# Seven products of quarter sums for the channel mixer's second product, with operand sums made on GpSimd

## The chip, the cores and the metric

The kernel runs on one core of a Trainium2 chip. The metric is the device time of one execution in microseconds (us); lower is better. A core has five engines with instruction streams of their own: PE (TensorE: matmuls, with PEld for its weight loads), DVE (VectorE), ACT (ScalarE), POOL (GpSimd) and SP (SyncE, which here issues DMAs). Work passes between them through SBUF, through PSUM (eight banks that matmuls accumulate in) and through DRAM.

## The reference, cut to what matters

The reference is one layer of a diffusion backbone: two token mixers (latent attention and a bidirectional recurrence), a merge, a channel mixer and a final norm, all in float32. The change touches the channel mixer, on 1024 rows of 1024 channels with an inner width of 2816:

```
u = h @ w_up                                  # 1024 x 5632
a, g = split(u, 2)
a = dwconv(a, ffn_conv_w, ffn_conv_b, 1, 1)   # three rows wide, each channel by itself
y = (silu(a) * g) @ w_down                    # 2816 -> 1024: the "second product"
x = x + g2 * y
out = rms_norm(x, final_g)
```

## The kernel before, in words

**Precision.** A float32 operand is split into a high part, rounded to fp32r by a copy on ACT, and a low part, the difference, by a subtraction on DVE (`split`, lines 119 to 122, and `high` and `low`, lines 1507 to 1518). Each product is then three matmuls: high by high, high by low, low by high.

**The first product** (h @ w_up) takes the 22 column tiles f of a and the 22 of g together, in a loop over f. It is already made of seven products of sums of quarters (Strassen's scheme in Winograd's form): for each f the left operands are sums of quarters of the weights (`wsum`, on DVE), the right operands are sums of quarters of h, made once, and seven products of 12 matmuls each (`times`, line 1548), in the order 1, 6, 5, 2, 7, 4, 3, accumulate in three PSUM banks. DVE and ACT combine the banks (`c_first`, `c_11` on ACT, and five sums `c_u2`, `c_u3`, `c_22`, `c_21`, `c_12` on DVE, line 1559) into `cpg[f]`, whose first half is a and whose second is g. While PE works on f, ACT and DVE finish f-1: convolution (`e_center`, `e_sides`, lines 1580 to 1585), `e_silu`, the gating (`e_gated`, line 1592), the split of the gated tile (`e_high`, `e_low`, lines 1596 and 1599), and a store of both parts to DRAM (`act_d`, issued on POOL, line 1600). They also prepare the operands for f+1. The order of all instructions of PE, DVE, ACT and SP is written out by hand in `channel_mixer`; each engine works through its own in that order, and what an engine waits for delays all that stands behind it on that engine. POOL has nothing to do in this stage but to issue the stores.

**The second product** (`Down`) works in two groups of four row tiles. For each group it goes through the 22 tiles f of the inner width: a step fetches half of the split activation and a weight tile (on SP), multiplies the weights by the gate row g2 (line 1801), splits them (line 122), and runs 24 matmuls (line 1812: four row tiles, two column halves, three part products) into eight PSUM banks. Three steps are prepared ahead. The last three f of each group are run tile by tile, so that the sum with x2 (line 1820), the norm and the store of a row tile (`final`) begin while PE is at the next tile. The second group's first tile uses the banks of the first group's first tile.

Of the kernel before, what the change touches and what calls it, by code (L numbers as in the profile page):

```python
# [106 lines left out]
class Block:  # L107
# [1378 lines left out]
    def setup_up(self):  # L1486
        self.ra, self.rg, self.s3, self.op, self.banks, self.p1, self.cpg, self.bt = ({} for _ in range(8))
        self.ups = None
        self.act_d = [self.tc.dram_tile([P, 2, T], F32, name=f"actd{f}") for f in range(NF)]
# [65 lines left out]
    def c_11(self, f):  # L1555
        self.nc.scalar.activation(self.cpg[f][:, 0, :512], self.bank(f, 1), AF.Copy)
# [4 lines left out]
    def c_u2(self, f):  # L1561
        self.c_sum(self.cpg[f][:, 0, 512:], self.p1[f], self.bank(f, 6))
# [4 lines left out]
    def c_22(self, f):  # L1567
        self.c_sum(self.cpg[f][:, 1, 512:], self.p1[f], self.bank(f, 5))

    def c_21(self, f):  # L1570
        self.c_sum(self.cpg[f][:, 1, :512], self.p1[f], self.bank(f, 4))

    def c_12(self, f):
        c = self.cpg[f][:, 0, 512:]
        self.c_sum(c, c, self.bank(f, 3))


    def e_center(self, f):
        self.ta = self.stage("ta")
        self.nc.scalar.activation(self.ta, self.cpg[f][:, 0, :], AF.Identity, bias=self.vec("fb", f), scale=self.vec("fw", 3 * f + 1))  # L1580

    def e_sides(self, f):
        c, ta, stt = self.cpg[f][:, 0, :], self.ta, self.nc.vector.scalar_tensor_tensor
# [6 lines left out]
    def e_gated(self, f):  # L1590
        g = self.cpg[f][:, 1, :]
        self.nc.vector.tensor_tensor(g, g, self.ta, op=OP.mult)

    def e_high(self, f):
        self.act = self.ups.tile([P, 2, T], F32R, tag="act", bufs=2, name=f"act{f}")
        self.nc.scalar.activation(self.act[:, 0, :], self.cpg[f][:, 1, :], AF.Copy)

    def e_low(self, f):
        self.nc.vector.tensor_tensor(self.act[:, 1, :], self.cpg[f][:, 1, :], self.act[:, 0, :].bitcast(F32), op=OP.subtract)  # L1599
        self.nc.gpsimd.dma_start(self.act_d[f], self.act.bitcast(F32))  # L1600

    def channel_mixer(self):
        tc, nc, a = self.tc, self.nc, self.a
        right_ctx, ups_ctx, down = ExitStack(), ExitStack(), Down(self)
        with tc.manual_schedule(engines=self.engines | {mybir.EngineType.SP}):
            cp = right_ctx.enter_context(self.pool("cpg", side="right"))
            h0, h1 = self.hf
            high, low, wsum = self.high, self.low, self.wsum

            def new_cpg(f):  # L1610
                self.cpg[f] = cp.tile([P, 2, T], F32, tag="cpg", bufs=2, name=f"cpg{f}")
# [16 lines left out]
            def first_sum(f):  # L1628
                new_cpg(f)
                self.p1[f] = self.cpg[f][:, 1, :512]  # L1630
                self.c_first(f)
# [53 lines left out]
            self.e_high(0)  # L1685
            low(2, 2)
            low(2, 7)
            self.e_low(0)
            high(2, 4)
            low(2, 4)  # L1690
            for f in range(2, NF):
# [5 lines left out]
                if not new:  # L1697
                    down.fetch_weights(0)
                    down.fetch_weights(1)
# [10 lines left out]
                if f > 2:  # L1710
                    first_sum(f)
                self.e_sides(f - 1)
                self.e_silu(f - 1)
# [4 lines left out]
                self.c_u2(f)  # L1718
                if new:
                    wsum(n, 7)  # L1720
                self.e_gated(f - 1)

                self.times(f, 2)
                self.e_high(f - 1)
# [4 lines left out]
                self.e_low(f - 1)  # L1729

                self.times(f, 7)
                self.c_11(f)
                if new:
# [20 lines left out]

            for n in range(3):
                down.fetch(n)
            down.fetch_weights(2)
# [7 lines left out]
            self.e_sides(f)  # L1765
            self.e_silu(f)
            down.prepare(3)
            self.e_gated(f)
            self.e_high(f)
            self.e_low(f)  # L1770
            ups_ctx.close()
            self.b_ctx.close()
            with self.pool("x2") as xp, self.pool("dn_ps", space=PSUM) as pp:
                down.run(xp, pp)
            right_ctx.close()


class Down:


    AHEAD, REST = 3, 3

    def __init__(self, b):
        self.b, self.nc = b, b.nc
        self.steps = [(g, f) for g in range(2) for f in range(NF)]
        self.acts, self.wds, self.raws = {}, {}, {}

    def fetch_weights(self, n):
        if n < len(self.steps):
            self.raws[n] = self.b.fetch(self.b.a["wdn"][self.steps[n][1]])  # L1790

    def fetch(self, n):
        if n < len(self.steps):
            g, f = self.steps[n]
            self.acts[n] = self.b.big(f"act{n}").rearrange("p (a b) -> p a b", a=2)
            self.nc.sync.dma_start(self.acts[n].bitcast(F32), self.b.act_d[f][:, :, g * 512:(g + 1) * 512])

    def prepare(self, n):
        if n < len(self.steps):
            raw = self.raws.pop(n)  # L1800
            self.nc.vector.tensor_tensor(raw, raw, self.b.g2r, op=OP.mult)
            wd = self.wds[n] = [self.b.big(f"wd{n}_{p}") for p in range(2)]
            self.b.split(raw, *wd)
            self.fetch_weights(n + 3)
            self.fetch(n + 3)

    def times(self, n, t, ps, cs=(0, 1)):
        f, act, wd = self.steps[n][1], self.acts[n], self.wds[n]
        for c in cs:
            p = ps[c]  # L1810
            for j, (rp, wp) in enumerate(((0, 0), (0, 1), (1, 0))):
                self.nc.tensor.matmul(p, act[:, rp, t * P:(t + 1) * P], wd[wp][:, c * 512:(c + 1) * 512],  # L1812
# [143 lines left out]
```

## Time and profile before

| | |
|---|---|
| median of 3 runs | 1943.05 us (1942.71 to 1944.17) |
| the profiled execution, its time | 1940.89 us |
| its span, first to last instruction | 1939.1 us |
| mean granted clock of TensorE | 0.987 |
| busy: PE, DVE, ACT, POOL | 1868.6, 1399.5, 926.2, 426.9 us |
| steady loop of the first product, one f | 19.5 us (84 matmuls) |
| second product, first matmul to end of the span | 1686.9 to 1939.1 us |

Rows of the profile give times in us from the start of the span, or mean durations in ns. A group of instructions is named by its source line, engine, operation and tiles, written first and read second. In rows of the kernel before, `cpg`, `op`, `act`, `wd` and `dn` are the combined tile, the split operands of the first product, the split activation, the split weights of the second product, and its PSUM banks.

### The profile page before, as it was taken

To read this page: it belongs to the slowest core of one execution; us is meant where nothing else is said; L and a number is where in the kernel's file an instruction comes from. 1 tells how busy PE (TensorE), PEld (TensorE's weight loads), DVE (VectorE), ACT (ScalarE), POOL (GpSimd) and SP (SyncE) were. 2 spreads that over 40 slices of the span, in tenths; PEclk is the share of its full clock that TensorE was granted. 3 is DMA by queue.
4 is the path that set the end of the run, shared out by engine and by line. 5 is a ranking of instruction groups with operands and counts; after the bars stand their busy time and mean duration, and the time that the engine had idled before them with its cause. 6 is when DMAs were issued, how large, how long until landed. Compare 5 with 4: busy or idle time off the path is not lost.

```text
span 1939.1 us, 21974 instructions
## 1 busy us (share of the span) xinstructions
PE 1868.6 (96%) x8272; PEld 1493.0 (77%) x8272; DVE 1399.5 (72%) x1613; ACT 926.2 (48%) x1218; POOL 426.9 (22%) x365
## 2 busy tenths in 40 slices
PE   7899999999999999999999899899999999999998
PEld 3688888878787877778777678677888888888786
DVE  6844678888888768777878765788777777664542
ACT  4434355656665646666666423444444444332221
POOL 2411402020202005666656400410000000000000
PEclk9999999999999999999999899999999999999999
DMA  8124633333332267333333481123232222486571
GB/s 331 55 94 164 227 112 114 114 115 131 116 144 83 94 227 235 95 120 114 119 97 133 129 314 44 55 76 123 95 117 101 113 105 109 166 325 224 195 261 44
DMA packets 96159, 272.78 MB, mean 141 GB/s; under 512 B 11937, under 2 KB 25011, under 8 KB 90934
## 3 DMA queue, kind: packets, MB, share of 16 engines
q1 hardware_dynamic: 77622, 189.22, 28.7%
q0 software_dynamic: 18000, 80.60, 10.8%
q10 hardware_dynamic: 432, 1.57, 0.2%
q8 instruction: 65, 1.06, 0.2%
q14 instruction: 40, 0.33, 0.1%
HBM read 196.49 MB, written 74.86 MB: 140 GB/s over the span
## 4 chain that ended last, share of the span: by engine, by line
PE 66%; DVE 15%; issue 9%; DMA 4%; POOL 3%; ACT 2%; SPq 0%; DVEq 0%; ACTq 0%; POOLq 0%
PE u L1548 21%; PE dn L1812 12%; PE f L1051 5%; PE z L160 5%; PE yo L160 5%; PE o L933 3%; PE f L160 2%; PE s L908 2%; PE s L909 2%; PE s L910 2%; DMA mw<-in_wmod_dram 1%; DVE wlo L122 1%; PE ya L160 1%; PE x L881 1%; PE g L160 1%
## 5 line engine op out<-in xcount | busy, mean ns | idle before, releaser
L1548 PE MATMUL u<-b,op 128*128 128x512 f32 x1320 | 317.1, 397 | 6.6 <-DVE op L1518 4.7
L1548 PEld LDWEIGHTS u<-b,op 128*128 128x128 f32 x1320 | 248.6, 189 | 68.7 <-DVE op L1518 6.2
L1812 PE MATMUL dn<-wd,act 128*128 128x512 f32 x1056 | 241.3, 391 | 2.4 <-DVE x L1820 2.4
L1812 PEld LDWEIGHTS dn<-wd,act 128*128 128x128 f32 x1056 | 199.2, 189 | 44.3 <-DVE x L1820 2.8
L160 PE MATMUL z<-hx,whi 128*128 128x512 f32 x736 | 210.7, 395 | 0.0
L927 POOL TENSOR_TENSOR acc<-acc,p 128x512 f32<-128x512 f32 x128 | 182.8, 1428 | 74.6 <-ACT p L914 71.2
L920 DVE TENSOR_TENSOR pl<-p,ph 128x512 fp32r<-128x512 f32 x160 | 168.4, 1057 | 23.9 <-ACT ph L916 23.6
L160 PE MATMUL f<-hx,whi 128*128 128x512 f32 x480 | 151.1, 396 | 0.0
L914 ACT ACTIVATE p<-s 128x512 f32<-128x512 f32 x160 | 95.6, 597 | 108.9 <-PE s L910 73.5
L160 PEld LDWEIGHTS z<-hx,whi 128*128 128x128 f32 x736 | 126.3, 188 | 25.4
L1548 PE MATMUL u<-h,op 128*128 128x512 f32 x528 | 132.8, 399 | 2.2 <-ACT cpg L1553 2.2
L1559 DVE TENSOR_TENSOR cpg<-cpg,u 128x512 f32<-128x512 f32 x102 | 70.1, 687 | 75.0 <-PE u L1548 74.2
L1548 PEld LDWEIGHTS u<-h,op 128*128 128x128 f32 x528 | 100.1, 191 | 25.3 <-ACT cpg L1553 2.7
L160 PE MATMUL z<-hx,wlo 128*128 128x512 f32 x368 | 115.6, 395 | 0.0
L122 DVE TENSOR_TENSOR wlo<-wraw,whi 128x1024 fp32r<-128x1024 f32 (+2 forms) x60 | 68.4, 1143 | 63.9 <-ACT whi L121 63.8
L121 ACT ACTIVATE wd<-wraw 128x1024 fp32r<-128x1024 f32 x44 | 46.7, 1061 | 137.7 <-PE dn L1812 72.2
L122 DVE TENSOR_TENSOR wd<-wraw,wd 128x1024 fp32r<-128x1024 f32 x44 | 53.9, 1225 | 80.3 <-ACT wd L121 78.3
L1051 PE MATMUL f<-l,whi 128*128 128x512 f32 x320 | 108.9, 396 | 0.0
L882 DVE TENSOR_REDUCE pm<-x 128x1 f32<-128x512 f32 x128 | 83.6, 683 | 35.0 <-PE x L881 25.5
L160 PEld LDWEIGHTS f<-hx,whi 128*128 128x128 f32 x480 | 90.0, 188 | 21.8 <-ACT r L463 0.3
L1600 POOL DMA_DIRECT2D actd<-act x22 | 11.8, 536 | 428.3 <-DVE act L1599 428.3
L916 ACT ACTIVATE ph<-p 128x512 fp32r<-128x512 f32 x160 | 101.2, 633 | 5.1
(335 smaller groups left out, 3811.9 us busy)
## 6 DMA issues: line engine op xcount, KB each, us to landing
actd<-act POOLq DMA_DIRECT2D x22, 1024.0 KB, 4.1
wraw<-in_wdn_dram SPq DMA_DIRECT2D x44, 512.0 KB
act<-actd SPq DMA_DIRECT2D x44, 512.0 KB
wraw<-in_wz_dram SPq DMA_DIRECT2D x41, 512.0 KB
mw<-in_wmod_dram POOLq DMA_DIRECT2D x32, 512.0 KB, 4.7
wraw<-in_wup_dram SPq DMA_DIRECT2D x23, 512.0 KB
lrud<-lruo POOLq DMA_DIRECT2D x10, 1024.0 KB, 4.6
l<-lrud SPq DMA_DIRECT2D x20, 512.0 KB
```

The source lines that it names most:

```text
L122: return self.nc.vector.tensor_tensor(lo, src, hi.bitcast(F32), op=OP.subtract)
L160: nc.tensor.matmul(ps, wts(k, wp), rhs(k, rp), start=(k == 0 and j == 0), stop=(k == nk - 1 and j == 2))
L882: nc.vector.tensor_reduce(r.pm[:, t, c:c + 1], ps, axis=mybir.AxisListType.X, op=OP.max)
L914: nc.scalar.activation(r.p[b], r.s.pop(b), AF.Exp, scale=SCALE)
L916: nc.scalar.activation(r.ph[b], r.p[b], AF.Copy)
L920: nc.vector.tensor_tensor(r.pl[b], r.p[b], r.ph[b].bitcast(F32), op=OP.subtract)
L927: nc.gpsimd.tensor_tensor(r.acc, r.p[0] if b == 1 else r.acc, r.p[b], op=OP.add)
L933: nc.tensor.matmul(r.o, r.v[b // 2][:, b % 2, :], pt.pop(b), start=(b == 0 and n == 0), stop=(b == NT - 1 and n == 1))
L1051: nc.tensor.matmul(f, (hi, lo)[wp][:, k * P:(k + 1) * P], lt[5 * j + k][rp][:, g * 512:(g + 1) * 512], start=(j == 0 and q == 0), stop=(j ...
L1548: self.nc.tensor.matmul(ps, w[wp][:, k * P:(k + 1) * P], self.right(i, k, rp), start=(first and k == 0 and j == 0), stop=(final and k == 3 ...
L1559: self.nc.vector.tensor_tensor(out, x, ps, op=OP.add)
L1812: self.nc.tensor.matmul(p, act[:, rp, t * P:(t + 1) * P], wd[wp][:, c * 512:(c + 1) * 512], start=(f == 0 and j == 0), stop=(f == NF - 1 a ...
```

## The change

The second product is now made of seven products of quarter sums as well. The activation (inner width by rows) and the weights (inner width by columns) are taken in pairs of inner tiles, 2k and 2k+1, which with the two halves of the rows and of the columns are four quarters each. For each of 11 pairs and seven products there is a left and a right operand, 128 by 512, kept in DRAM.

- In the first product's loop the split and the store of the gated tile go. Its tile `cpg` becomes two, `c` and `pg`; `pg` alternates between two pools, so that it lives for four f in place of two. For each f, SP stores the first half of `pg` (`e_quarter`); for each pair, POOL makes four sums of quarters and issues three stores (`e_sums`, in even f). In eleven of the iterations (`chains`) SP fetches two weight tiles (`w_fetch`) and POOL multiplies them by g2, makes five sums and issues five stores (`w_sums`). POOL's order is written out by hand now too.
- In f = 2, `c_u2` is moved ahead, and `e_silu` and `e_gated` of f = 1 are moved behind `c_11`.
- `Down` goes through 77 steps, the products in the order 1, 6, 2, 5, 7, 3, 4 and 11 pairs in each. A step fetches a left and a right operand side by side into one tile, splits it, and runs 12 matmuls (four row tiles, three part products). Products 1, 2, 7, 4 use four banks, 6, 5, 3 the other four; during a product's first steps the banks of the product before it are read (`after`), two row tiles' work in a step. x2 is fetched in the first eight steps. The last five steps are run tile by tile.

```diff
+        self.left_d = {1: quarters("da1"), 2: quarters("da2"), 7: quarters("da7"), 6: first(self.a65), 5: second(self.a65),
+                       3: first(self.a34), 4: second(self.a34)}
+        self.right_d = {1: quarters("db1"), 2: quarters("db2"), 6: quarters("db6"), 5: first(self.b57), 7: second(self.b57),
+                        4: first(self.b43), 3: second(self.b43)}
...
-    def e_high(self, f):
-        self.act = self.ups.tile([P, 2, T], F32R, tag="act", bufs=2, name=f"act{f}")
-        self.nc.scalar.activation(self.act[:, 0, :], self.cpg[f][:, 1, :], AF.Copy)
-
-    def e_low(self, f):
-        self.nc.vector.tensor_tensor(self.act[:, 1, :], self.cpg[f][:, 1, :], self.act[:, 0, :].bitcast(F32), op=OP.subtract)
-        self.nc.gpsimd.dma_start(self.act_d[f], self.act.bitcast(F32))
+    def e_quarter(self, f):
+
+        self.nc.sync.dma_start(self.left_d[1 + f % 2][f // 2], self.pg[f][:, :512])
+
+    def e_sums(self, k):
+
+        nc, (x, y) = self.nc, (self.pg.pop(f) for f in (2 * k, 2 * k + 1))
+        s3 = self.stage("s3")[:, :512]
+        a11, a21, a12, a22 = x[:, :512], x[:, 512:], y[:, :512], y[:, 512:]
+        tt, sub = nc.gpsimd.tensor_tensor, OP.subtract
+        tt(s3, a11, a21, op=sub)
+        nc.gpsimd.dma_start(self.left_d[7][k], s3)
+
+        tt(a21, a21, a22, op=OP.add)
+        tt(a11, a21, a11, op=sub)
+        nc.gpsimd.dma_start(self.a65[k], x)
+        tt(a12, a12, a11, op=sub)
+        nc.gpsimd.dma_start(self.a34[k], y)
+
+    def w_fetch(self, k):
+        self.wd = [self.ups.tile([P, D], F32, tag="wdr", bufs=2, name=f"wdr{2 * k + e}") for e in range(2)]
+        for e in range(2):
+            self.nc.sync.dma_start(self.wd[e], self.a["wdn"][2 * k + e])
+
+    def w_sums(self, k):
+
+        nc, (x, y) = self.nc, self.wd
+        b11, b12, b21, b22 = x[:, :512], x[:, 512:], y[:, :512], y[:, 512:]
+        tt, sub = nc.gpsimd.tensor_tensor, OP.subtract
+        tt(x, x, self.g2r, op=OP.mult)
+        nc.gpsimd.dma_start(self.right_d[1][k], b11)
+        tt(y, y, self.g2r, op=OP.mult)
+        nc.gpsimd.dma_start(self.right_d[2][k], b21)
+        tt(b11, b12, b11, op=sub)
+        tt(b12, b22, b12, op=sub)
+        nc.gpsimd.dma_start(self.b57[k], x)
+        tt(b21, b21, b22, op=sub)
+        tt(b21, b21, b11, op=OP.add)
+        nc.gpsimd.dma_start(self.b43[k], y)
+        tt(b11, b22, b11, op=sub)
+        nc.gpsimd.dma_start(self.right_d[6][k], b11)
...
-        with tc.manual_schedule(engines=self.engines | {mybir.EngineType.SP}):
+        with tc.manual_schedule(engines=self.engines | {mybir.EngineType.SP, mybir.EngineType.Pool}):
             cp = right_ctx.enter_context(self.pool("cpg", side="right"))
+            chains = {3: 0, 5: 1, 7: 2, 9: 3, 11: 4, 12: 5, 13: 6, 15: 7, 17: 8, 19: 9, 21: 10}
...
-                self.cpg[f] = cp.tile([P, 2, T], F32, tag="cpg", bufs=2, name=f"cpg{f}")
+                self.c[f] = cp.tile([P, T], F32, tag="c", bufs=2, name=f"c{f}")
+                self.pg[f] = (cp if f % 4 < 2 else self.ups).tile([P, T], F32, tag="pg", bufs=2, name=f"pg{f}")
...
                 self.times(f, 7)
                 self.c_11(f)
+                if f == 2:
+                    self.e_silu(1)
+                    self.e_gated(1)
+                    self.e_quarter(1)
+                if f % 2 == 0:
+                    self.e_sums(f // 2 - 1)
+                if f in chains:
+                    self.w_sums(chains[f])
...
+    ORDER = 1, 6, 2, 5, 7, 3, 4
+    AHEAD, REST, PAIRS = 3, 5, NF // 2
...
     def prepare(self, n):
         if n < len(self.steps):
...
+            self.parts[n] = [self.b.big(f"dp{n}_{p}") for p in range(2)]
+            self.b.split(self.raws.pop(n), *self.parts[n])
+            self.fetch(n + (3 if self.xp is None else 5))
+
+    def times(self, n, t):
+        i, k = self.steps[n]
+        parts, ps = self.parts[n], self.bank[i][t]
+        first, final = i in (1, 6, 5, 7), i in (2, 3, 4, 6)
+        for j, (lp, rp) in enumerate(((0, 0), (0, 1), (1, 0))):
+            self.nc.tensor.matmul(ps, parts[lp][:, t * P:(t + 1) * P], parts[rp][:, 512:], start=(first and k == 0 and j == 0),
+                                  stop=(final and k == self.PAIRS - 1 and j == 2), skip_group_check=True)
...
+            for t in range(4):
+                self.times(n, t)
+            for step in islice(pending, 2):
+                step()
+            if n < 8:
+                nc.sync.dma_start(x2[n], b.x2_d[n])
```

## Rows read from the trace of the kernel before

**Rows 1.** The page's first part: busy us, share of the span, instructions.
```profile
PE 1868.6 (96%) x8272; PEld 1493.0 (77%) x8272; DVE 1399.5 (72%) x1613; ACT 926.2 (48%) x1218; POOL 426.9 (22%) x365
```

**Rows 2.** Windows: stretch, its length, busy by engine, granted clock, DMA share, GB/s.
```profile
1300.00:1304.40 4.40, 3.59 (x9) 2.85 (x10) 3.78 (x6) 2.44 (x3) 0.57 (x1) 0.61 0.58 238
1467.00:1667.00 200.00, 200.00 (x862) 161.54 (x862) 154.37 (x208) 86.50 (x122) 5.34 (x10) 1.00 0.28 108
1686.91:1930.80 243.89, 241.33 (x1057) 199.04 (x1055) 125.51 (x120) 60.27 (x68) 0.53 (x1) 0.99 0.59 213
...
1840.00:1860.00 20.00, 20.00 (x90) 16.53 (x89) 11.80 (x10) 4.63 (x6) 0.00 (x0) 1.00 0.99 382
1800.00:1820.00 20.00, 17.61 (x71) 14.09 (x71) 10.10 (x15) 5.40 (x10) 0.00 (x0) 0.91 0.37 131
```

**Rows 3.** Waits of PE from 1280 us on: total us, times, longest.
```profile
PE dn L1812 <- DVE x L1820: 2.4, 1, 2.4
PE u L1548 <- ACT cpg L1553: 2.2, 1, 2.2
PE u L1548 <- DVE cpg L1559: 1.0, 1, 1.0
```

**Rows 4.** Timeline of one f: start, us, engine, what [idle before, releaser].
```profile
1471.51 0.33 SPq L1620 DMA_DIRECT2D graw<-in_wup_dram  x1
1471.89 0.42 SPq L126 DMA_DIRECT2D wraw<-in_wup_dram  x1
1472.19 2.95 PE L1548 MATMUL u<-h,op 128*128 128x512 f32 x12
...
1478.03 0.69 DVE L1559 TENSOR_TENSOR cpg<-cpg,u 128x512 f32<-128x512 f32 x1 [0.98 <-PE u L1548]
...
1486.31 1.41 DVE L1559 TENSOR_TENSOR cpg<-cpg,u 128x512 f32<-128x512 f32 x2 [2.29 <-PE u L1548]
```

**Rows 5.** Groups of DVE, 1320 to 1680 us: busy us, mean ns, idle before.
```profile
L1559 DVE TENSOR_TENSOR cpg<-cpg,u 128x512 f32<-128x512 f32 x91 | 62.6, 688 | 69.0 <-PE u L1548 68.4
L1518 DVE TENSOR_TENSOR op<-wraw,op 128x512 fp32r<-128x512 f32 x72 | 47.9, 685 | 0.0
...
L1599 DVE TENSOR_TENSOR act<-cpg,act 128x1024 fp32r<-128x1024 f32 x19 | 23.3, 1225 | 1.1 <-ACT act L1596 1.1
```

**Rows 6.** Timeline ahead of the loop, where DVE and POOL both subtract.
```profile
1242.14 1.30 POOL L1505 TENSOR_TENSOR wraw<-wraw 128x512 f32<-128x512 f32 x1
...
1260.09 1.61 POOL L1640 TENSOR_TENSOR hf<-hf 128x512 f32<-128x512 f32 x1
1260.48 1.76 DVE L1472 TENSOR_TENSOR hf<-hf 128x512 f32<-128x512 f32 x1
...
1261.65 1.73 POOL L1638 TENSOR_TENSOR hf<-hf,hf 128x512 f32<-128x512 f32 x1
1262.16 1.76 DVE L1518 TENSOR_TENSOR op<-g1raw,op 128x512 fp32r<-128x512 f32 x1
```

**Rows 7.** Groups of DVE in attention, 724 to 1090 us.
```profile
L882 DVE TENSOR_REDUCE pm<-x 128x1 f32<-128x512 f32 x120 | 78.3, 683 | 23.5 <-PE x L881 23.1
```

**Rows 8.** Groups of POOL over the span.
```profile
L1600 POOL DMA_DIRECT2D actd<-act x22 | 11.8, 536 | 428.3 <-DVE act L1599 428.3
...
L611 POOL TENSOR_TENSOR zr<-zr,cos 128x1024 f32<-128x1024 f32 x2 | 4.8, 2410 | 6.4 <-issue 4.8 <-DVE zr L610 1.5
```

**Rows 9.** Timeline where the second product begins.
```profile
1686.91 33.28 PE L1812 MATMUL dn<-wd,act 128*128 128x512 f32 x146
...
1700.81 1.22 DVE L1592 TENSOR_TENSOR cpg<-cpg,ta 128x1024 f32<-128x1024 f32 x1
```

**Rows 10.** The tail: L1812's matmuls after 1800 us, and the last of DVE.
```profile
L1812 PE MATMUL dn<-wd,act x558: 387/389/796, 1799.8 to 1930.2; 128*128 128x512 f32 x186
...
1934.63 1.41 DVE L1840 SCALAR_TENSOR_TENSOR o<-x,last,g0r 128x512 f32<-128x512 f32 x2
```

**Rows 11.** DMA issues: queue, count, KB each, median us to landing.
```profile
x2d<-xt POOLq DMA_DIRECT2D x8, 512.0 KB, 2.9
```

More of the change, by code (lines that the diff above doesn't have):

```diff
@@ L1555, in c_11 @@
     def c_11(self, f):
[L1556 removed]
+        self.nc.scalar.activation(self.c[f][:, :512], self.bank(f, 1), AF.Copy)
     def c_sum(self, out, x, ps):
@@ L1561, in c_u2 @@
     def c_u2(self, f):
-        self.c_sum(self.cpg[f][:, 0, 512:], self.p1[f], self.bank(f, 6))
+        self.c_sum(self.c[f][:, 512:], self.p1[f], self.bank(f, 6))
     def c_u3(self, f):
@@ L1778 @@
 class Down:
-    AHEAD, REST = 3, 3
+    ORDER = 1, 6, 2, 5, 7, 3, 4
+    AHEAD, REST, PAIRS = 3, 5, NF // 2
     def __init__(self, b):
         self.b, self.nc = b, b.nc
[L1785 to L1790, printed above, removed]
+        self.steps = [(i, k) for i in self.ORDER for k in range(self.PAIRS)]
+        self.raws, self.parts, self.xp = {}, {}, None
@@ L1798, in prepare @@
+            self.nc.sync.dma_start(raw[:, :512], b.left_d[i][k])
+            self.nc.sync.dma_start(raw[:, 512:], b.right_d[i][k])
     def prepare(self, n):
         if n < len(self.steps):
[L1800 to L1812, printed above, removed]
-                                      start=(f == 0 and j == 0), stop=(f == NF - 1 and j == 2))
@@ new lines, in run @@
+        for n in range(7, 9):
+            self.fetch(n)
+        tile = lambda n: pp.tile([P, 512], F32, name=n)
+        one = [tile(f"da{t}") for t in range(4)]
+        two = [tile(f"db{t}") if t < 2 else b.fp.tile([P, 512], F32, tag="f", bufs=2, name=f"db{t}") for t in range(4)]
+        self.bank = {1: one, 2: one, 7: one, 4: one, 6: two, 5: two, 3: two}
+        x2 = self.x2 = [xp.tile([P, D], F32, name=f"x2_{t}") for t in range(T // P)]
+        u = xp.tile([P, 4, 512], F32, name="u")
+        tt = nc.vector.tensor_tensor
@@ new lines, in run @@
+        self.ss = {}
+        pending = iter(())
+        last = len(self.steps) - self.REST
+        for n in range(last):
+            i, k = self.steps[n]
+            if n:
+                self.prepare(n + self.AHEAD)
+            if k == 0 and n:
+                pending = after(self.ORDER[self.ORDER.index(i) - 1])
+            for t in range(4):
[4 more added lines that the diff above has]
+                nc.sync.dma_start(x2[n], b.x2_d[n])
+            if n == 8:
+                nc.sync.dma_start(b.g1r, b.a["rows"][4:5].to_broadcast([P, D]))
@@ new lines, in run @@
+        for step in pending:
+            step()
+        for n in range(last + self.AHEAD, len(self.steps)):
+            self.prepare(n)
+        for t in range(4):
+            for n in range(last, len(self.steps)):
+                self.times(n, t)
+            add(4 + t, left, one[t])
+            x = x2[4 + t]
+            s = self.half_square(4 + t, 0)
+            nc.vector.tensor_scalar(self.ss[t], self.ss[t], 1.0 / D, EPS, op0=OP.mult, op1=OP.add)
+            nc.scalar.activation(s, s, AF.Sqrt, bias=self.ss[t], scale=1.0 / D)
+            nc.vector.reciprocal(s, s)
+            o = xp.tile([P, D], F32, tag="o", bufs=2, name=f"o{4 + t}")
+            for c in (left, right):
+                nc.vector.scalar_tensor_tensor(o[:, c], x[:, c], s, b.g1r[:, c], op0=OP.mult, op1=OP.mult)
+                nc.sync.dma_start(b.out[(4 + t) * P:(5 + t) * P, c], o[:, c])
```

150 lines of the change are left out of this document (70 added, 80 removed).

## The prediction

> **What bounds the kernel now.** I read the page first: TensorE is busy for 96% of the span [rows 1], so only fewer matmuls, or fewer gaps between them, can shorten the kernel. Next came the windows [rows 2]. In the 200 us of the first product's steady loop TensorE never pauses while VectorE works 154.4 us of it, and in the second product (1686.91 to 1930.80) TensorE again works almost throughout. Third, the waits of TensorE [rows 3]: from 1280 us to the end there are only four, of 2.4, 2.2 and 1.0 us and a last one of 0.8 that I leave out of the sums. The 2.4 us is where the second product's first row group ends: the window around it has a granted clock of 0.91, which is (1 - 0.91) x 20 us = 1.8 us lost at the lower level, 1.2 GHz, just after that gap. So the path is TensorE in both stages, and VectorE is the engine close behind it in the first. The reader should then look at one turn of the loop over f [rows 4], where every idle time of VectorE before its work says how late it may be.
>
> **The second product: what is removed.** Before: 22 f x 2 groups x 24 = 1056 matmuls in 243.89 us [rows 2]. Less the gap of 2.4 and the 1.8 for the clock behind it this is 239.7 us, or 0.227 us each. After: 7 products x 11 pairs x 4 tiles x 3 = 924 matmuls of the same shape, 209.7 us. Saved: 30.0 us.
> The gap of 2.4 us and the clock loss behind it (together 4.2 us) go as well: the products alternate between two sets of four banks (1, 2, 7, 4 in one, 6, 5, 3 in the other), and each bank is read during the product after, on VectorE and ScalarE with time to spare.
> The tail: before, the last matmul ends at about 1930.6 (start 1930.2 [rows 10], and one lasts 0.4) and the last VectorE operation at 1934.63 + 1.41 = 1936.04, 5.4 us later, because the last tiles queue up behind whole-row scaling. After, each of the last four tiles has 15 matmuls (3.4 us) ahead of one half-row add (0.7), a square with its read-out (0.7), a root and a reciprocal (0.5) and two half scalings (1.4), 3.4 us in all, which keeps pace. The tail becomes 3.4 us: 2.0 saved. What follows 1936.04 stays.
> VectorE's work per matmul falls: the weight multiply goes from the second product, and a step of 12 matmuls (2.7 us) needs one subtraction of the 1225 ns kind [rows 5] and now and then two adds of 0.68. It is prepared three steps ahead (8 us), which covers the adds. Loads are 512 KB a step as against 1 MB for 24 matmuls: the same rate, 193 GB/s, half of the 382 that one window reached [rows 2].
>
> **The start of the second product.** SP issues the store of f=21's first quarter ahead of the loads for step 7 and on. That store waits for the gating. Before, the gating ended at 1700.81 + 1.22 = 1702.0, 15.1 us after the product began [rows 9]. After, three multiplies of 1.22 and the high copy no longer stand ahead of it: about 1696.4, 9.5 us in. Steps 0 to 6 (19 us of TensorE) live on loads issued earlier, so the wait itself is covered. From there 10 steps of loads, 8 row tiles of x2 and GpSimd's last sums are 10.75 MB, 28.1 us at 382 GB/s: the last of these is due at about 1728 and lands at about 1727. Cover of one or two us; I put 1 us for this place (0 if the rate holds, 5 if it is 320).
>
> **The first product: what moves to GpSimd.** Removed from each f: the high copy on ScalarE and the low subtraction (1225 ns [rows 5]) on VectorE. Added on GpSimd for each pair: four tensor operations 512 wide (e_sums), and in eleven iterations two 1024 wide and five 512 wide (w_sums), with eight DMA issues of 0.54 us [rows 8]. GpSimd alone has time: 9 x 1.3 [rows 6] + 2 x 2.4 [rows 8] + 8 x 0.54 = 20.8 us in a pair's 39 us. The question is what it does to VectorE.
> The trace has the answer in some 25 us where both ran subtractions [rows 6]. Alone, a 512-wide subtraction takes 0.68 us on VectorE [rows 5] and 1.30 on GpSimd. Side by side VectorE's takes 1.76 and GpSimd's 1.61 to 1.73, and their ends alternate: GpSimd ends at 1261.70, VectorE at 1262.24, GpSimd at 1263.38, VectorE at 1263.92. They take turns, 1.68 us for one of each, 1.1 for GpSimd and 0.58 for VectorE: whichever comes second waits until the other has ended. I carry that over to widths that no row pairs, 1024 columns among them. A VectorE reduction that reads PSUM alone keeps its 683 ns in attention, where GpSimd is adding [rows 7]; sums with one operand in PSUM (L1559) I count as free of it too.
> The Trainium skill, SBUF — State Buffer, section "SBUF: two separate sides", says that a VectorE operation with two SBUF inputs and a GpSimd operation exclude one another for a whole instruction. The 1.68 us turns agree for 512 columns; no row shows a 1024-wide pair. By it a VectorE operation behind a 1024-wide multiply waits its full time; if the two shared instead, I would halve the loss below to some 8 us.
>
> Of VectorE's work in one iteration all but the five L1559 sums reads two SBUF operands. GpSimd holds the turn 4 x 1.1 = 4.4 us in e_sums and 2 x 2.4 + 5 x 1.1 = 10.3 us in w_sums. VectorE's idle time is 45.6 of 200 us [rows 2], 4.5 in an iteration of 19.5, and 1.2 more without the low subtraction: 5.7. So e_sums fits. w_sums need not: from below it costs nothing, if its holds fall into idle time and PSUM sums; from above 10.3 - 5.7 = 4.6 us each, 51 us over eleven.
> To choose I lay it along the order of the code, counting from the iteration's first matmul (1472.19 in [rows 4]). SP issues the gate and up loads at -0.7 and -0.3 and now two weight loads right behind. At 2.9 us to landing for the first 512 KB [rows 11] and 1.37 for each further one at 382 GB/s, the weights land at 5.0 and 6.4. GpSimd's first multiply holds 5.0 to 7.4; the sum L1559 at 5.84 passes; wsum 7 runs to 8.0, the gating to 9.2 while GpSimd issues its DMA; the second multiply holds to 11.6; wsum 5 to 12.2, low 1 to 12.8 (a DMA issue); then turns: 13.9, wsum 6 14.5, 15.6, low 5 16.2; the two PSUM sums (at 14.1 and 14.8 before [rows 4]) end at 17.6. Product 3 starts at 16.7 and accumulates on the bank that the second of them reads: TensorE waits 0.9 us. If the weights land 1 us sooner or later, other operations fall behind the multiplies and the same count gives 1.5 to 2.0. I take 1.3. VectorE then enters the even iteration some 3 us late; there e_sums starts after the gating, and the lateness is gone by the same bank (16.3 against 16.7).
> Six iterations (5, 7, 9, 11, 17, 19) at 1.3: 8 us. At f = 12 to 15 three w_sums follow each other and e_sums comes between, so VectorE meets GpSimd all the time; the same laying-out gives waits at the PSUM sum after product 6 (1.8) and at c_11 (1.2), and about 3 in the next two: 6 us. f=21 prepares no next f: 0. At f=2 and 3 the wait of 2.2 us [rows 3], for the buffer that the low part's store held, goes; but the gating of f=1 now stands behind c_11, with wsum 6, low 5 and both PSUM sums behind it on VectorE, so it comes back before products 4 and 3, and f=3's w_sums meets a VectorE that is late: 3 us more than before. Sum: 17 us lost in the first product.
>
> **The sum.** -30.0 - 4.2 - 2.0 + 1 + 17 = -18.2 us. The profiled execution took 1940.89 us with a span of 1939.1; its 1940.9 becomes 1923. The median of the runs is 2.2 us above the profiled one, and I forecast for it: 1943.05 - 18 = 1925 us.
>
> **Rivals.** (A) VectorE absorbs the turns: only f=2 and 3 cost 3 us, and the time is 1943 - 35 + 3 = 1911. For it speaks idle time of 5.7 us in each iteration; against it that only 3.3 of this stands ahead of the bank's due time. (B) Slower: the waits in the w_sums iterations reach about 2.2 us. The waits of 2.2 and 2.4 us [rows 3] were each followed by the lower clock (0.61 over 4.4 us behind the first, 0.91 over 20 us around the second [rows 2]), which costs some 1.8 us more; 4.0 x 11 = 44 us is more than the 35 that the second product gives, so 1943 - 35 + 44 = 1952. It decides from 35 / 11 = 3.2 us an iteration, clock included. Against it stands my 1.3, which is nearer to the wait of 1.0 [rows 3]. (C) The second product starves at its start, loads at 320 GB/s: 5 us in place of 1, 1929. (D) The seven products do not pay at all, because a matmul gets slower with a bank change every three: for that 924 matmuls would need 0.26 us each; the first product changes its banks only every 12, so no row excludes it, but before, the second product already changed after every three, at 0.227.
>
> **How the numbers follow.** Forecast, with first-product losses of 8 to 28 us: 0.60. A 0.18, C 0.06, B 0.12, and 0.04 for a loss that just eats the gain. Faster by over 0.2%: 0.60 + 0.18 + 0.06 = 0.84; within 0.2% (3.9 us, about what a measurement of this kernel tells from no change) 0.04; slower 0.12. The range goes from A without its 3 us (1908) to a loss of 34 us in the first product (1942), which leaves out B and the edge of A.
>
> **What would show it.** Right: 924 matmuls at 0.227 us with no gap at a product's change; VectorE operations of two SBUF operands at 1.7 us or more beside GpSimd's, L1559 sums still at 0.69; waits of TensorE of about 1 us for the PSUM sums (c_22) in odd f, none in even; a tail of 3.4 us after the last matmul. Wrong: no waits in odd f (A), the lower clock in every odd f (B), TensorE waiting for the split of steps 9 to 16 (C), or a multiply that VectorE does not wait for.

## The result and the profile after

The change makes the kernel slower: 1970.74 us, the median of four runs (1966.98 to 1975.43), against 1943.42 for the kernel before (1942.71 to 1944.17). The ratio is 1.0142 with a 95% interval of 1.0119 to 1.0165. The forecast was 1925 with a range of 1908 to 1942; rival B, the one on the slower side, had put it at 1952. The profiled execution took 1971.78 us with a span of 1970.0.

The page's first part, for the kernel after (answers to [rows 1]):

```profile
PE 1859.6 (94%) x8140; PEld 1477.7 (75%) x8140; DVE 1524.0 (77%) x1606; ACT 937.3 (48%) x1239; POOL 668.1 (34%) x552
```

There are 132 matmuls fewer, as planned. VectorE, from which the low subtraction and the multiplies by g2 were taken, is busy for 125 us more: its operations have become longer. Busy time here contains the time for which an operation that was asked for waits its turn with GpSimd.

Windows of the kernel after (columns as in [rows 2]): the first product from 1280 us on, three even and three odd f of its steady loop (504 matmuls), and the second product.

```profile
1280.00:1750.88 470.88, 426.09 (x1742) 334.45 (x1740) 438.37 (x400) 154.15 (x230) 246.06 (x204) 0.96 0.41 154
...
1386.05:1521.24 135.19, 123.16 (x505) 97.36 (x505) 126.75 (x115) 44.52 (x66) 68.50 (x58) 0.96 0.40 152
...
1750.88:1970.00 219.12, 210.54 (x925) 173.24 (x924) 132.52 (x142) 97.81 (x116) 6.85 (x5) 0.99 0.66 229
```

And one window of the kernel before, the same part of the first product:

```profile
1280.00:1686.91 406.91, 402.75 (x1723) 323.76 (x1721) 312.51 (x416) 176.26 (x247) 11.25 (x21) 1.00 0.29 112
```

The second product, to the end of the span, takes 219.1 us against 252.2 (1686.9 to 1939.1): 33.1 saved, where -30.0 - 4.2 - 2.0 + 1 = -35.2 was forecast. The first product takes 64.0 us longer, of which 3.7 is no work of the change: the loop over f begins 3.7 us later in this execution (1264.3 against 1260.6), a lag that is there before any changed instruction. Of the other 60.3 TensorE idles for 44.8 - 4.2 = 40.6, and 23.3 - 3.7 = 19.6 is TensorE being busy for longer at the lower clock. The row of six f says the same: 12.0 us of pauses in 135.2, where [rows 2] had none in 200, with VectorE at work or in its turn for 94% of the time.

The waits of TensorE from 1280 us on, kernel after (answers to [rows 3]):

```profile
PE u L1556 <- DVE pg L1567: 35.2, 17, 3.7
PE u L1556 <- ACT c L1564: 4.8, 5, 2.0
PE u L1556 <- ACT pg L1561: 2.4, 1, 2.4
PE u L1556 <- DVE c L1567: 2.2, 3, 1.2
PE da L1864 <- DVE dp L122: 1.2, 2, 0.8
PE da L1864 <- ACT dp L121: 0.5, 1, 0.5
```

The place is the one that the prediction named: product 3's bank, which VectorE's PSUM sum (L1567, L1559 before) reads late. Only the size differs: 2.8 us in most odd f where 1.3 was forecast, and 2.2 and 2.6 in two even ones (f = 8 and 18) where none was. Eight stretches at 1.2 GHz, some 34 us together, lie in this loop; seven of them begin within or behind waits of 2.2 us or more, though four waits of 2.4 to 2.8 us were not followed by one. Here is the wait of f=8 and, as a window, the product behind it, 12 matmuls that take 4.61 us where those behind the wait of f=7 took 3.06:

```profile
1453.00 4.61 PE L1556 MATMUL u<-b,op 128*128 128x512 f32 x12 [2.23 <-DVE pg L1567]
```

```profile
1453.00:1457.45 4.45, 4.45 (x13) 3.50 (x14) 3.55 (x6) 0.00 (x0) 0.00 (x0) 0.62 0.30 87
```

Groups of VectorE from 1320 to 1720 us, kernel after (answers to [rows 5]):

```profile
L1526 DVE TENSOR_TENSOR op<-wraw,op 128x512 fp32r<-128x512 f32 x70 | 92.4, 1340 | 2.7 <-ACT op L1522 2.7
...
L1526 DVE TENSOR_TENSOR op<-graw,op 128x512 fp32r<-128x512 f32 x35 | 60.5, 1730 | 0.0
...
L1567 DVE TENSOR_TENSOR pg<-pg,u 128x512 f32<-128x512 f32 x52 | 35.3, 679 | 0.6
```

The subtraction with two SBUF operands that took 685 ns [rows 5] takes 1340 to 1730 on average. The sum with one operand in PSUM keeps its 679.

The timeline of f=7, whose first matmul is at 1411.29, kernel after, from the moment the weights have landed:

```profile
1418.32 3.49 POOL L1631 TENSOR_TENSOR wdr<-wdr,g1r 128x1024 f32<-128x1024 f32 x1 [11.33 <-DMA wdr<-in_wdn_dram]
1418.34 1.22 DVE L1600 TENSOR_TENSOR pg<-pg,ta 128x1024 f32<-128x1024 f32 x1
1419.47 2.89 DVE L1513 TENSOR_TENSOR graw<-graw 128x512 f32<-128x512 f32 x1
...
1422.12 0.60 POOL L1632 DMA_DIRECT2D db<-wdr  x1 [0.30 <-POOL wdr L1631]
1422.29 3.42 DVE L1526 TENSOR_TENSOR op<-wraw,op 128x512 fp32r<-128x512 f32 x1
...
1422.73 2.41 POOL L1633 TENSOR_TENSOR wdr<-wdr,g1r 128x1024 f32<-128x1024 f32 x1
1425.45 0.58 POOL L1634 DMA_DIRECT2D db<-wdr  x1 [0.30 <-POOL wdr L1633]
1425.74 2.17 DVE L1513 TENSOR_TENSOR wraw<-graw,wraw 128x512 f32<-128x512 f32 x1
1426.05 1.30 POOL L1635 TENSOR_TENSOR wdr<-wdr 128x512 f32<-128x512 f32 x1
1427.43 1.61 POOL L1636 TENSOR_TENSOR wdr<-wdr,wdr 128x512 f32<-128x512 f32 x1
1427.83 1.76 DVE L1526 TENSOR_TENSOR op<-graw,op 128x512 fp32r<-128x512 f32 x1
...
1429.51 1.39 DVE L1567 TENSOR_TENSOR pg<-pg,u 128x512 f32<-128x512 f32 x2
...
1430.96 0.73 PE L1556 MATMUL u<-b,op 128*128 128x512 f32 x2 [2.79 <-DVE pg L1567]
```

Read it as pairs of lines. GpSimd begins 7.0 us into the iteration, not 5.0. A 512-wide subtraction behind the 1024-wide multiply takes 2.89 and 3.42 us in place of 0.68. The one at 1422.29 is asked for while GpSimd issues its DMA (1422.12 to 1422.72), and yet it ends only at 1425.71, 0.57 us behind the multiply that GpSimd starts afterwards; the one at 1425.74 does the same (it ends at 1427.91, 0.56 behind the subtraction that began at 1426.05). So an issue that has another of GpSimd's operations behind it did not let VectorE in; between 1300 and 1745 us this holds for 41 of the 42 VectorE operations, PSUM sums apart, that came up during such an issue. The two PSUM sums, free of all this themselves, stand behind these operations in VectorE's order, and TensorE waits 2.79 us for the second.

### The profile page after: what moved, and what is told of

Its sections match the earlier page's. It is cut to its first block, busy times and chain, and to the rows that moved or that the text cites. A ratio compares the mean times of both kernels' runs of the same rounds, so it can differ in the third digit from the quotient of the medians.

```text
span 1970.0 us, 22262 instructions
## 1 busy us (share of the span) xinstructions
PE 1859.6 (94%) x8140; PEld 1477.7 (75%) x8140; DVE 1524.0 (77%) x1606; ACT 937.3 (48%) x1239; POOL 668.1 (34%) x552
## 4 chain that ended last, share of the span: by engine, by line
PE 61%; DVE 24%; issue 7%; ACT 3%; DMA 3%; POOL 1%; SPq 0%; DVEq 0%; ACTq 0%; POOLq 0%
PE u L1556 11%; PE z L160 9%; PE f L1051 5%; DVE op L1526 5%; PE yo L160 5%; PE db L1864 5%; PE da L1864 4%; PE f L160 4%; PE o L933 3%; PE g L160 3%; PE s L910 2%; PE s L908 2%; PE s L909 2%; PE x L881 1%; DVE pg L1567 1%
## 5 line engine op out<-in xcount | busy, mean ns | idle before, releaser
L1556 PE MATMUL u<-b,op 128*128 128x512 f32 x1320 | 336.8, 411 | 46.7 <-DVE pg L1567 35.2
L1556 PEld LDWEIGHTS u<-b,op 128*128 128x128 f32 x1320 | 256.6, 196 | 119.8 <-DVE pg L1567 43.0
L1522 ACT ACTIVATE op<-wraw 128x512 fp32r<-128x512 f32 x90 | 56.0, 626 | 182.0 <-DVE wraw L1513 158.0
L122 DVE TENSOR_TENSOR dp<-dr,dp 128x1024 fp32r<-128x1024 f32 x77 | 94.5, 1250 | 39.2 <-ACT dp L121 38.4
L121 ACT ACTIVATE dp<-dr 128x1024 fp32r<-128x1024 f32 x77 | 81.3, 1063 | 86.2 <-DMA dr<-db 65.2
L122 DVE TENSOR_TENSOR wlo<-wraw,whi 128x1024 fp32r<-128x1024 f32 (+2 forms) x60 | 68.5, 1144 | 64.4 <-ACT whi L121 64.4
L1526 DVE TENSOR_TENSOR op<-wraw,op 128x512 fp32r<-128x512 f32 x90 | 113.6, 1282 | 5.2 <-ACT op L1522 5.1
L1864 PE MATMUL da<-dp,dp 128*128 128x512 f32 x352 | 108.8, 390 | 1.2 <-DVE dp L122 1.2
L160 PE MATMUL f<-hx,wlo 128*128 128x512 f32 x240 | 94.9, 396 | 0.0
```

Source lines behind the costliest of these rows:

```text
L121: self.nc.scalar.activation(hi, src, AF.Copy)
L122: return self.nc.vector.tensor_tensor(lo, src, hi.bitcast(F32), op=OP.subtract)
L160: nc.tensor.matmul(ps, wts(k, wp), rhs(k, rp), start=(k == 0 and j == 0), stop=(k == nk - 1 and j == 2))
L1526: self.nc.vector.tensor_tensor(lo, self.left(f, i), hi.bitcast(F32), op=OP.subtract)
L1556: self.nc.tensor.matmul(ps, w[wp][:, k * P:(k + 1) * P], self.right(i, k, rp), start=(first and k == 0 and j == 0), stop=(final and k == 3 ...
L1864: self.nc.tensor.matmul(ps, parts[lp][:, t * P:(t + 1) * P], parts[rp][:, 512:], start=(first and k == 0 and j == 0), stop=(final and k == ...
```

## The experiments

Each kernel is the changed one with the edit shown, on the same chip as runs of the kernel before, whose medians lay between 1941.6 and 1945.4. Where one time is given, the kernel ran once, and a few us between two such times mean little: the four runs of the changed kernel lie within 8.5 us, and in the traces the loop over f begins anywhere from 1259.9 to 1265.1 us, ahead of anything that an edit touches. So "the first product" below is its length in the trace, from the loop's begin (1264.3 in the kernel after) to the second product's first matmul (1751.4): 487.1 us after the change, 426.3 before it.

**1. and 2. Without the sums, with their stores.** `w_sums` keeps its DMA issues and loses its seven operations; in the second kernel those of `e_sums` go as well.

```diff
-        tt(x, x, self.g2r, op=OP.mult)
         nc.gpsimd.dma_start(self.right_d[1][k], b11)
-        tt(y, y, self.g2r, op=OP.mult)
...
-        tt(b11, b22, b11, op=sub)
```

> Leaves out the seven tensor operations of w_sums on GpSimd (multiplies and sums of the weights); its fetches and its five stores stay. Theory (turns): GpSimd's tensor operations hold VectorE up in the first product, so with the larger part of them gone the time falls to about 1920 us, and the waits of TensorE in odd f vanish. Rival (traffic): the larger DMA traffic and the stores on GpSimd's queue are late and hold the loop up; then it stays at 1960 or above.

> Leaves out all tensor operations on GpSimd in the first product's loop (those of e_sums too); all fetches and stores stay, with the data unsummed. Turns: the first product is back to its length before, and the time is that of the second product's saving alone, about 1943 - 33 = 1910 us, or 1913 if the new order at f = 2 costs what was forecast. Traffic: above 1950.

Measured: 1911.7 and 1905.86 us. The window of six f of the steady loop (504 matmuls) in each, the first kernel's first:

```profile
1390.00:1507.02 117.02, 117.02 (x505) 94.54 (x504) 99.14 (x115) 45.57 (x66) 30.71 (x37) 1.00 0.49 184
```

```profile
1390.00:1507.02 117.02, 117.02 (x506) 94.51 (x504) 83.43 (x115) 45.49 (x67) 15.59 (x29) 1.00 0.53 195
```

The weights and stores still move (184 and 195 GB/s against 152 after), and TensorE does not pause: the traffic costs nothing. The operations of `w_sums` cost 59 us by the times and 60.3 by the first product (487.1 against 426.8). Those of `e_sums` alone cost 6 by the times, but 2.9 of these lie ahead of the loop; the first product gives 1.4 (426.8 against 425.4).

**3. What of an operation keeps VectorE waiting.** Each of GpSimd's operations becomes three writes of a constant, which read nothing.

```diff
+    def thrice(self, out, x, y, op):
+        for _ in range(3):
+            self.nc.gpsimd.memset(out, 0.5)
...
-        tt, sub = nc.gpsimd.tensor_tensor, OP.subtract
+        tt, sub = self.thrice, OP.subtract
```

> Each tensor operation of e_sums and w_sums is replaced by three constant fills of its output on GpSimd (the stored sums are constants): GpSimd is busy in the same places and waits for the same loads and stores, but reads nothing from SBUF. If VectorE waits only for a GpSimd operation that reads SBUF, the time is that without sums, 1906 to 1912. If any work of GpSimd holds it up, it stays above 1930.

Measured: 1906.18 us. The same six f, and a group, of this kernel:

```profile
1390.00:1507.02 117.02, 117.02 (x505) 94.56 (x504) 83.40 (x115) 45.48 (x67) 70.71 (x120) 1.00 0.50 184
```

```profile
L1526 DVE TENSOR_TENSOR op<-wraw,op 128x512 fp32r<-128x512 f32 x72 | 47.9, 685 | 0.0
```

GpSimd is as busy in six f as after the change (70.7 us against 68.5), and VectorE's subtraction is back at 685 ns. Work of GpSimd's that reads no SBUF does not disturb VectorE; its reading does. (The fills are also shorter turns, 0.53 us for 512 columns; experiment 7 shortens turns that do read, and gains nothing.) The Trainium skill, SBUF — State Buffer, section "SBUF: two separate sides", says this of a VectorE operation with two SBUF inputs: that it and a GpSimd operation exclude each other only where the latter reads SBUF, and that whichever starts first has the shared ports for its whole instruction. This run agrees, and so do the 2.89 us of the subtraction that was asked for during the first multiply above. The one of 3.42 us does not fit: it came up before its multiply began, during the issue, and ended behind it all the same.

**4. The issues out of the way.** All stores of a group of sums are issued behind its last operation.

```diff
-        nc.gpsimd.dma_start(self.right_d[1][k], b11)
         tt(y, y, self.g2r, op=OP.mult)
-        nc.gpsimd.dma_start(self.right_d[2][k], b21)
...
         tt(b11, b22, b11, op=sub)
+        nc.gpsimd.dma_start(self.right_d[1][k], b11)
+        nc.gpsimd.dma_start(self.right_d[2][k], b21)
```

> All tensor operations stay, but in e_sums and w_sums the stores are issued after the last of them (so some stores take later values than they should). If a DMA issue on GpSimd between two tensor operations keeps VectorE out as well, as the first trace suggests (a VectorE operation that asks during the issue runs only after the next GpSimd operation), the time falls by 10 to 25 us, to 1945 to 1960. If issues cost VectorE nothing, it stays at 1970.

Measured: 1963.28 us, 7.5 less than after, between what the two theories gave; the first product takes 480.9 us, 6.2 less. Its waits and the window of two f (168 matmuls):

```profile
PE u L1556 <- DVE pg L1567: 25.3, 13, 3.0
PE u L1556 <- ACT c L1564: 8.8, 8, 2.0
```

```profile
1424.27:1467.99 43.72, 41.12 (x168) 32.51 (x168) 40.01 (x39) 14.97 (x22) 23.19 (x19) 0.96 0.43 157
```

The wait for product 3's bank falls from 2.8 to 2.1 us in most odd f, and those of f = 8 and 18 go, but waits of 0.5 to 1.5 us for `c_11` come in the same odd f, and of 1.5 and 2.1 us in f = 4 and 6. All waits in the first product fall from 44.6 to 39.3 us. VectorE's busy time in two f falls from 42.3 to 40.0 us. The issues are a part of the loss, and a small one.

**5. The order at f=2.** The special places of f=1's gating are undone.

```diff
-                else:
-                    self.c_u2(f)
...
-                if f > 2:
-                    self.e_silu(f - 1)
+                self.e_silu(f - 1)
...
```

> The order at f = 2 as before the change (sum after product 6, activation and gating of f = 1 in their old places); all else as changed. If the new order is what costs at f = 2 and 3 (waits of 1.2, 2.0, 1.6 and 3.6 us there), the time falls by 4 to 10 us, to about 1963; if these waits come from GpSimd's turns as elsewhere, it stays within 3 us of 1970.

Measured: 1971.99 us, the first product 487.6. This order costs nothing that one run can show.

**6. A smaller burst.** `w_sums` without its two 1024-wide multiplies.

```diff
-        tt(x, x, self.g2r, op=OP.mult)
-        tt(y, y, self.g2r, op=OP.mult)
```

> Leaves out the two 1024-wide multiplies of w_sums; its five 512-wide sums stay. They hold 4.8 of the 10.3 us. If the loss goes with the time held, the 59 us that w_sums cost fall by about half, to 1940. If what counts is the number of turns (seven against five), it falls by 17 us, to 1954. If a due time is missed or kept as a whole, with nothing between, the time is below 1920.

Measured: 1922.25 us. Against 1905.86 without any sums the loss is 16 us where it was 65: two operations of eleven hold some three quarters of it. None of the three values came out, and the last is nearest: the loss falls by far more than the time held. The waits left are 0.9 us in most odd f, and only two stretches at the lower clock remain. The window of eight f (672 matmuls) of this kernel:

```profile
1355.34:1516.21 160.87, 157.29 (x672) 125.86 (x672) 143.10 (x153) 59.73 (x88) 70.47 (x70) 1.00 0.47 177
```

**7. Shorter turns.** The same multiplies, each as four of 256 columns.

```diff
-        tt(x, x, self.g2r, op=OP.mult)
+        for c in range(0, D, 256):
+            tt(x[:, c:c + 256], x[:, c:c + 256], self.g2r[:, c:c + 256], op=OP.mult)
```

> Each 1024-wide multiply on GpSimd as four of 256 columns; all else as changed, the same columns are held. If a VectorE operation waits for one whole instruction and then has its turn, shorter turns let VectorE through four times as often and the time falls by 10 to 30 us. If only the sum of the time held counts, it stays at 1970 or rises by the instructions' overhead.

Measured: 1970.36 us, nothing gained; the first product takes 488.6 us. The window of four f (336 matmuls):

```profile
1404.25:1493.00 88.75, 82.29 (x336) 65.06 (x336) 82.12 (x77) 29.74 (x44) 50.16 (x50) 0.96 0.41 154
```

VectorE is busy for 41.1 us in two f where it was 42.3. A multiply of 256 columns takes 0.73 us at the least, four of them 2.9 where the whole takes 2.41, so more time was held in all: the run shows that shorter turns do not make up for that, not that a turn's length is without effect.

**8. The burst begun sooner.** The weights are loaded in the even iteration before, so that GpSimd goes on from `e_sums` to `w_sums` without a pause.

```diff
-                if f in chains:
+                if f in (12, 13):
                     self.w_fetch(chains[f])
...
+                if f % 2 == 0 and f != 12 and f + 1 in chains:
+                    self.w_fetch(chains[f + 1])
```

> As the changed kernel, but the two weight loads of each w_sums are issued in the middle of the even iteration before, not at the start of its own (f = 12 and 13 apart), so that GpSimd's burst begins before the odd iteration does. Theory that the lateness of the burst against product 3's bank costs the time: the waits of 2.8 us in odd f fall below 2 or go to even f, fewer stretches at the lower clock, 1925 to 1950 us. Theory that VectorE simply gives up more time in a pair than it has idle: the waits move but their sum stays, 1960 to 1972.

Measured: 1959.12 us, a hair below what the second theory gave. The waits of this kernel from 1467 to 1667 us, and the window of four f (336 matmuls):

```profile
PE u L1556 <- ACT pg L1561: 5.9, 4, 1.7
PE u L1556 <- DVE pg L1567: 5.6, 2, 3.7
PE u L1556 <- ACT c L1564: 2.8, 5, 0.6
PE u L1556 <- DVE c L1567: 2.6, 4, 0.7
```

```profile
1418.48:1504.59 86.11, 80.19 (x337) 62.46 (x337) 82.08 (x77) 29.87 (x44) 46.42 (x38) 1.00 0.43 160
```

TensorE's pauses are cut into pieces of 1.67, 0.65 and 0.55 us in a pair of iterations, but from 1280 to 1740 us they sum to 39.5 us where the changed kernel has 44.4 (460 less TensorE's busy time). Three stretches at the lower clock are left of eight. Those three last 10 us together where the eight last 34, and half of the difference, 12 us, is all that the first product gained (475.2 us against 487.1). So the place of the burst sets how the waits are cut and what the clock adds, and their sum only a little.

**9. Both at once.** Experiments 4 and 8 together.

> As the kernel whose weights are loaded an iteration sooner (1959.1 us, TensorE waiting 2.9 us in a pair), and its stores are issued after the last operation of each group of sums, so that what some of them store is not what the second product needs; the time alone is looked at. Theory that an issue between two of GpSimd's operations keeps VectorE waiting as the operations do (about 0.87 us with the pause before it, seven or eight in a pair): the waits in a pair fall from 2.9 us by most of that, 1915 to 1940 us. Theory that only the operations' own time counts: 1953 to 1961.

Measured: 1947.86 us, between the two theories: 11 us less than experiment 8, 8 of them in the first product (466.9 us). The window of four f:

```profile
1413.22:1497.43 84.21, 79.70 (x336) 62.44 (x337) 79.90 (x77) 29.85 (x44) 47.82 (x39) 1.00 0.44 163
```

TensorE waits 2.3 us in a pair where the window of experiment 8 has 3.0. An issue counts, but for a fraction of the 0.87 us that the first theory gave it.

**10. and 11. The same sums on VectorE.** The operations go one by one into VectorE's order, GpSimd issues the stores; in the first kernel the last pair stays on GpSimd, in the second all eleven move, and two steps at f=2 and f=21 stand later. In both the weights of the pairs are spread evenly, one pair to each odd f from 3 to 19 and the last two at f=21 and at the second product's start, where the changed kernel had three in f = 11 to 13. The second kernel also places its first splits of the second product anew.

```diff
+    def w_step(self, k, j):
...
+        nc.vector.tensor_tensor(out, p, q, op=op)
+        if j not in (2, 4):
+            nc.gpsimd.dma_start(...)
...
-                    self.w_sums(chains[f])
+                    for j in range(2):
+                        self.w_step(chains[f], j)
```

> The same sums for ten of the eleven pairs on VectorE, one or two at each place where it sat idle before (behind low 3, behind the convolution, behind low 5), their stores still issued on GpSimd; the last pair stays on GpSimd, at the start of the second product. Theory (turns): VectorE pays 0.6 us for each 512 columns and never waits for GpSimd, 7.7 us a pair inside 11.4 us of idle time; the first product then has hardly a wait and the time is that without any sums, 1906, plus 3 to 10 us: 1909 to 1916. Rival (VectorE is full): the idle time is needed for the hand-overs with ScalarE and TensorE, and VectorE's own sums cost TensorE as much as GpSimd's did, 1945 or more.

> All eleven pairs' sums on VectorE. The last pair's are put between the splits of steps 4 to 9, the sum of f=21 that waited 5 us for a store is moved behind the PSUM sums, and the two of f=2 too. By the first trace with sums on VectorE these three places cost TensorE 6, 2 and 1 us and two stretches at the lower clock. Turns: with no tensor operation left on GpSimd the time comes to 1906 to 1912. If the waits at the second product's start come from its loads rather than from GpSimd's turns, they stay and the time is 1917 or more.

Measured: 1919.08 us (1915.55 to 1924.31), ratio 0.9879 (0.9853 to 0.9905), and 1915.09 us (1913.04 to 1919.81), ratio 0.9863 (0.9838 to 0.9888). Both are 3 us above what the theory of turns gave. The first rival, VectorE full at 1945 or more, is out; the second, loads at the second product's start, comes back below. The six f of the first:

```profile
1390.00:1507.02 117.02, 117.02 (x506) 94.52 (x505) 107.06 (x148) 45.47 (x67) 13.00 (x24) 1.00 0.47 176
```

VectorE now does all of GpSimd's operations besides its own and is busy for less time than with GpSimd's help (107.1 us against 126.8 in six f), and TensorE does not pause. Its first product takes 433.2 us, that of the second kernel 426.5, as before the change. Most of what is left in the second kernel stands in one row of its waits, where the second product starts; the window after it shows the DMA engines full and the clock down:

```profile
PE db L1927 <- ACT dp L121: 4.7, 1, 4.7
```

```profile
1735.00:1750.00 15.00, 13.42 (x47) 10.48 (x48) 10.20 (x9) 10.68 (x12) 0.00 (x0) 0.77 1.05 387
```

**12. The loads of x2 later.** The kernel of experiment 11, with the 4 MB of x2 (and the row of the last scale) taken from the second product's first steps, where they stood among the operands, to steps 12 to 20.

```diff
-            if n < 8:
-                nc.sync.dma_start(x2[n], b.x2_d[n])
+            if 12 <= n < 20:
+                nc.sync.dma_start(x2[n - 12], b.x2_d[n - 12])
```

> As the kernel with all pairs' sums on VectorE, but the loads of x2 and of the last scale in the second product are issued at its steps 12 to 20 in place of 0 to 8. If the 4.7 us that TensorE waited there, and the lower clock behind it (0.77 over 15 us, 3.5 us), came from these 4 MB standing ahead of the operands of step 9, both go: 1915 - 7 = 1908 us (1905 to 1911). If the last pair's sums or the stores set that wait, it stays: 1913 to 1917.

Measured: 1906.83 us (1903.63 to 1907.6), ratio 0.9806 (0.9786 to 0.9826). Of TensorE's waits in the second product this is left:

```profile
PE da L1927 <- DVE dp L122: 0.4, 1, 0.4
```

The wait of 4.7 us is gone. Of the versions that leave out no work this is the fastest that was run, 64 us below the changed kernel and 38 below the kernel before; it shows what the second product's saving is worth once GpSimd's turns are out of the way.

## Why the prediction was wrong

**What held.** Nearly all of the second product. Matmuls: 924 at about 0.228 us, the gap in its middle and the clock loss behind it gone. The tail: the last matmul ends at 1963.14 and VectorE at 1966.60, 3.5 us later, where 3.4 was forecast (its parts add up to 3.3). The start cost 1.7 us of waits where 1 was forecast, but that is luck: 1.3 of them are waits for the split of the very first step (at 1751.4 and 1752.7 us), and only 0.45, at 1780.8 us, lie at a step that the loads in question feed. The sum of these loads in the prediction is also too small: 21.5 loads of 512 KB at its own 1.37 us are 29.5 us, not 28.1, and leave no cover. Rival D falls with this, and rival A with the waits. Rival C's starving start did not show in the changed kernel. In experiment 11 the start did wait, 4.7 us where C gave 5, but not for C's reason, loads at 320 GB/s: the DMA engines moved 387, and experiment 12 shows that the 4 MB of x2 in their way were the cause.

**The step that failed** is the laying-out of the w_sums iteration, with its term "17 us lost in the first product", which measured 60. Its mechanism, turns between VectorE and GpSimd with a late PSUM sum in front of product 3, was right, and so was the size of the holds. What was wrong was how much of them VectorE would not feel. VectorE's busy time in the windows shown, for an even and an odd f together, shows it (us):

```
own work, GpSimd reads nothing (exp. 3)    83.40 / 3 = 27.8
with e_sums on GpSimd (exp. 1)             99.14 / 3 = 33.0
with e_sums and w_sums (the change)       126.75 / 3 = 42.3
the same sums on VectorE (exp. 10)        107.06 / 3 = 35.7
what TensorE needs for the two f          117.02 / 3 = 39.0
```

The prediction held 4.4 us for e_sums and 10.3 for w_sums, and VectorE lost 5.2 and 9.2, 14.5 in all (126.75 less 83.40, over 3) for 14.7. Some 2.3 of the 14.5 go with the issues (experiment 4 has 40.0 for the 42.3), so about 12 of the 14.7 us of turns were waited out, with little credit for idle time and PSUM sums. The prediction instead let turns run out there, and counted "So e_sums fits" for the even iteration by itself. Alone e_sums did fit (1.4 us, experiments 1 and 2); behind a w_sums it did not. Over the two f its own numbers give 39.0 - 2 x 5.7 = 27.6 us of VectorE's work and 14.7 of holds, 42.3 us, more than 39.0. It would have been the better sum. Its upper bound of 51 us for eleven iterations would have been nearer too: 40.6 us of waits, where the forecast had 17, and 19.6 of clock, where it had nothing, make 60.

**The smaller errors inside that step.** "The gating to 9.2 while GpSimd issues its DMA" and "low 1 to 12.8 (a DMA issue)" took an issue for a gap in which VectorE gets its turn; the timeline shows that it is none where another operation follows, and moving the issues gave 7.5 us (experiment 4) and 11 (experiment 9), in the first product 6 and 8. "The weights land at 5.0" was 7.0, and why is open; experiment 8 shows that an earlier landing by itself mostly moves the waits and thins out the stretches at the lower clock. "The lateness is gone by the same bank" did not hold at f = 8 and 18, with waits of 2.2 and 2.6 us. No lower clock was counted in the forecast; it costs 17 to 20 us (half of 34, or the 19.6 above), and experiment 8, which leaves most of the waits and takes away five of the eight stretches, is 12 us faster.

**Rival B** had the mechanism, both parts of the price (2.2 us and 1.8 for the clock) and the point of 3.2 us from which it decides; measured are 60.3 / 11 = 5.5 us an iteration. It was given 0.12 because the wait of 1.3 was taken from a laying-out that had left out the terms above.

**What stays open.** Experiment 6 has VectorE at 143.10 / 4 = 35.8 us for the two f, less than 39.0, and still waits of 0.9 us and a first product of 443.3 us; experiment 10, with the same 35.7, has 433.2. Experiments 4 and 9 both have 40.0, and first products of 480.9 and 466.9. So where in the iteration the turns fall also matters, and how much of the loss is shortage and how much is place was not separated. Nor is it known why an issue between two operations costs less than its own length.

## What to carry to other kernels

Before work is moved to GpSimd to relieve VectorE, add the full length of GpSimd's operations that read SBUF to VectorE's own time over a whole period, with no credit for idle time, and compare it with what TensorE needs; here 42.3 against 39.0 would have told the sign. A sum below what TensorE needs is no promise, as experiment 6 shows (35.8, and still 16 us lost). Then price the other choice, the same operations on VectorE: they cost it 7.9 us in two f, where GpSimd's help cost it 14.5. A wait costs more than its length where the clock drops behind it: here 40.6 us of waits brought 19.6 us at the lower clock with them, so a loss can grow faster than its cause.

## What the runs showed of the hardware

Three things were not expected. A VectorE operation with two SBUF operands that is asked for while GpSimd issues a DMA ends behind GpSimd's next operation, where one that reads SBUF follows at once (2.17 and 3.42 us for 0.68). GpSimd operations that only write left such operations at 685 ns, beside 70.7 us of GpSimd work in 117. And a multiply of 1024 columns cut into four of 256 gained nothing (1970.36 us against 1970.74), with 2.9 us for the four where the whole takes 2.41.
